# The attention output product of a mixer by seven products, its gate pairs regrouped, and the first three rows of w_o interleaved

## The chip, the cores and the metric

One core of a Trainium2 chip runs the whole program: TensorE (PE) multiplies, VectorE (DVE), ScalarE (ACT) and GpSimd (POOL) do the element work, and SyncE (SP) issues most of the loads. The metric is the device time of one execution in microseconds. Before the change the median of three executions is 2502.44 us (2501.37 to 2502.45).

## What is computed

Two layers of a macaron block over 640 tokens (512 of a new stream, 8 x 16 of running streams), 1024 features, float32:

```python
x += 0.5 * swiglu(rmsnorm(x) * g1, w_ffn1)
h  = rmsnorm(x) * gm
z  = h @ w_in                       # conv B | C | V | q | k | v | gates (2 x 1024)
y_conv = B * causal_conv3(C * V)    # 512 features
y_attn = band_attention(q, k, v)    # 512 features
m  = sigmoid(g_c) * (y_conv @ w_conv_out) + sigmoid(g_a) * (y_attn @ w_attn_out)
x += m @ w_o
x += 0.5 * swiglu(rmsnorm(x) * g2, w_ffn2)
```

and a last norm. The change lies in the computation of `m` and in `m @ w_o`.

## The kernel before

Everything is kept transposed: features on the 128 partitions, tokens (T = 640, in two halves of HT = 320) along the free dimension. Features come in tiles of 128 (KT = 8 of the model's width, CT = 4 of the conv's and of the attention's). Float32 products are made of three matmuls: each operand is split in a rounded part `hi` and a rest `lo`, and hi·hi + lo·hi + hi·lo is summed in PSUM. Weights arrive by SP in raw slabs of 128 x 1024 (`load`, a ring of three buffers); `prep` casts a slab to `whi` on ACT, and `flush` computes `wlo = raw - whi` on VectorE (L311). Both have rings of three.

Many products are done **by seven**: a product of 2 x 2 blocks (the two token halves, and odd and even feature tiles) is formed from seven block products instead of eight. The seven operands are named X11, X21, XN6, XT5, XT7, X22, XT4; those with N or T are sums of halves of the input. The weights' sums are made on VectorE in `source` (L250, four adds for a pair of slabs), whose results are split like raw slabs. One such stretch uses four slabs, s0 to s3, with two blocks of 12 matmuls in each of the first three and one in the last.

`outputs` is the part at issue. It holds, in this order, gate pairs 2, 4 and 6 (`gate_pair(m)`: rows m and m + 1 of the gates by seven, 84 matmuls into three PSUM banks qa, qb, qc); two `unit`s, which compute four rows each of y_conv @ w_conv_out by seven (84 matmuls; A and B are two-bank tiles, C two single banks); then gate pairs 8, 10, 12 and 14, and after each of these two rows of y_attn @ w_attn_out in the plain way (`out`, 48 matmuls a row, `py`). For gates from 8 on (`direct`), VectorE adds the blocks straight out of PSUM; for the others ACT copies a block to a scratch tile (`capsm`, `c`) and a DMA issued from POOL adds it (`accumulate`). `scale` multiplies a gate by the norm's factor `rrm`, `bend` is the sigmoid on ACT, `weigh` multiplies a row of the conv result by its gate, and `give` splits rows of `m` into hi and lo for w_o. Jobs are attached to numbered places of a pair or unit with `at(place, i, job)`; `spot` runs them there.

In this part the order on TensorE, VectorE and ACT is the one in which the program is written (`manual_schedule`, ORDERED), and each engine takes its queue strictly in that order, so an operation that waits holds up what is written behind it. The rows of `m @ w_o` follow: `product(po, mo)` for m = 0 to 7, 48 matmuls each, which need all eight rows of `mo` in turn; then x[m] is updated, and the next norm and the FFN's operands are begun (`ex.weights`, `ex.final`).

`mixer_order` lists the same pieces for the host, which packs the weights in the order of their use; `kinds` derives the slabs from it.

## Time and profile before

| | |
|---|---|
| median of three executions | 2502.44 us |
| the profiled execution | 2501.53 us |
| its span, from the first to the last instruction | 2499.7 us |
| granted TensorE clock | 0.999 |
| from gate pair 8 to the first row of w_o, layer 0 | 704.83 to 782.36 us |
| the same, layer 1 | 1940.3 to 2017.9 us |
| POOL busy in the first of these stretches | 0.00 us |

Times in the views count from the span's start. A row of the timeline gives start, length, engine, line, operation, result and operands, and in brackets the idle time before it with what ended that. Rows that overlap by some 0.08 us on one engine follow each other without a gap, so what an operation costs its engine is the distance from its start to the next one's. [...] The windows give an engine's busy time in a stretch. The chain is the work that ended last, followed back from the end.

### The profile page before, as it was taken

Reading aid. Unit: us, or ns where it says so; the run is one execution under the profiler, and the core shown is the slowest. Engines: PE = TensorE matmul, PEld = TensorE weight load, DVE = VectorE, ACT = ScalarE, POOL = GpSimd, SP = SyncE. Lnnn points to the kernel's source line nnn. Section 1 sums busy time; section 2 is a strip of 40 time slices with the busy share of each in tenths; the row PEclk is TensorE's granted clock in tenths of the full one; section 3 lists DMA queues with packets and bytes.
Section 4 is the critical chain, followed back from the end, with each engine's and each line's share of the span. In section 5 each row is a group of like instructions: output and inputs, shape, how many; then the busy total and the mean of one; then the engine's idle time right before and its main releaser. Section 6 shows DMA issues by size and latency. Waiting matters only on the chain.

```text
span 2499.7 us, 43407 instructions
## 1 busy us (share of the span) xinstructions
PE 2483.1 (99%) x17096; PEld 2425.8 (97%) x17096; DVE 2103.9 (84%) x3304; ACT 1418.8 (57%) x2281; POOL 335.3 (13%) x407
## 2 busy tenths in 40 slices
PE   9999999999999999999999999999999999999998
PEld 8999999888999999999999999998899999999998
DVE  7888888878886899888798889888788868989887
ACT  7455556664654555555565555556646455555554
POOL 0011211211100011111001111121111000111111
PEclk9999999999999999999999999999999999999999
DMA  4245665335323344666435565643344233565564
GB/s 146 82 109 122 138 138 130 108 108 172 101 76 112 95 119 119 137 135 135 114 92 128 129 133 121 138 119 117 132 145 107 78 114 94 119 132 120 131 135 111
DMA packets 127021, 299.59 MB, mean 120 GB/s; under 512 B 12160, under 2 KB 70912, under 8 KB 126816
## 3 DMA queue, kind: packets, MB, share of 16 engines
q1 hardware_dynamic: 68976, 219.18, 27.8%
q0 software_dynamic: 57120, 76.98, 18.5%
q8 instruction: 134, 2.20, 0.4%
q10 hardware_dynamic: 720, 0.65, 0.1%
q14 instruction: 71, 0.58, 0.1%
HBM read 221.13 MB, written 7.94 MB: 92 GB/s over the span
## 4 chain that ended last, share of the span: by engine, by line
PE 94%; DVE 3%; ACT 2%; DMA 0%; issue 0%; SPq 0%; DVEq 0%
PE pab L396 12%; PE paa L396 11%; PE pcb L396 6%; PE pca L396 6%; PE daa L963 5%; PE dab L963 5%; PE po L373 4%; PE qa L396 4%; PE pbb L396 3%; PE pba L396 3%; PE dca L963 3%; PE dcb L963 3%; PE pda L373 2%; PE pv L1589 2%; PE ma_cv L396 2%; PE qc L396 2%
## 5 line engine op out<-in xcount | busy, mean ns | idle before, releaser
L311 DVE TENSOR_TENSOR wlo<-raw,whi 128x1024 fp32r<-128x1024 f32 (+1 forms) x575 | 593.7, 1035 | 222.9 <-ACT whi L306 217.4
L306 ACT CAST whi<-raw 128x1024 fp32r<-128x1024 f32 (+1 forms) x575 | 515.6, 900 | 349.3 <-PE pbb L396 44.6
L306 ACT CAST whi<-s 128x1024 fp32r<-128x1024 f32 (+1 forms) x160 | 151.1, 945 | 246.5 <-issue 107.9
L396 PE MATMUL pab<-xhib,whi 128*128 128x320 f32 x704 | 218.3, 310 | 0.4 <-DVE gb L250 0.4
L396 PE MATMUL pab<-xlob,whi 128*128 128x320 f32 x704 | 217.4, 309 | 0.0
L396 PE MATMUL pab<-xhib,wlo 128*128 128x320 f32 x704 | 217.4, 309 | 0.0
L396 PE MATMUL paa<-xhia,whi 128*128 128x320 f32 x640 | 198.1, 310 | 0.2 <-DVE ga L250 0.2
L396 PE MATMUL paa<-xloa,whi 128*128 128x320 f32 x640 | 197.7, 309 | 0.0
L396 PE MATMUL paa<-xhia,wlo 128*128 128x320 f32 x640 | 197.7, 309 | 0.0
L311 DVE TENSOR_TENSOR wlo<-s,whi 128x1024 fp32r<-128x1024 f32 (+1 forms) x160 | 174.0, 1088 | 10.6 <-ACT whi L306 10.6
L396 PEld LDWEIGHTS pab<-xhib,whi 128*128 128x128 f32 x704 | 132.1, 188 | 1.1 <-DVE gb L250 0.9
L396 PEld LDWEIGHTS pab<-xlob,whi 128*128 128x128 f32 x704 | 132.1, 188 | 0.2
L396 PEld LDWEIGHTS pab<-xhib,wlo 128*128 128x128 f32 x704 | 132.1, 188 | 0.0
L396 PEld LDWEIGHTS paa<-xhia,whi 128*128 128x128 f32 x640 | 120.2, 188 | 0.5 <-DVE ga L250 0.5
L396 PEld LDWEIGHTS paa<-xloa,whi 128*128 128x128 f32 x640 | 120.1, 188 | 0.1
L396 PEld LDWEIGHTS paa<-xhia,wlo 128*128 128x128 f32 x640 | 120.1, 188 | 0.0
L250 DVE TENSOR_TENSOR raw<-raw,raw 128x512 f32<-128x512 f32 x160 | 109.5, 684 | 1.3
L250 DVE TENSOR_TENSOR raw<-s,raw 128x512 f32<-128x512 f32 x160 | 109.7, 686 | 0.0
L396 PE MATMUL pcb<-xhib,whi 128*128 128x320 f32 x352 | 108.7, 309 | 0.0
L396 PE MATMUL pcb<-xlob,whi 128*128 128x320 f32 x352 | 108.7, 309 | 0.0
L396 PE MATMUL pcb<-xhib,wlo 128*128 128x320 f32 x352 | 108.7, 309 | 0.0
L987 POOL DMA_DIRECT2D x<-c_b x52 | 62.6, 1204 | 309.7 <-ACT c_b L980 134.6
(705 smaller groups left out, 8073.0 us busy)
## 6 DMA issues: line engine op xcount, KB each, us to landing
raw<-in_wst SPq DMA_DIRECT2D x375, 512.0 KB, 3.7
x<-c_b POOLq DMA_DIRECT2D x52, 320.0 KB, 5.0
x<-c_a POOLq DMA_DIRECT2D x50, 320.0 KB, 5.1
kc<-in_kcache SPq DMA_DIRECT2D x32, 256.0 KB, 3.7
vc<-in_vcache SPq DMA_DIRECT2D x16, 512.0 KB, 4.5
ub<-cbb POOLq DMA_DIRECT2D x42, 160.0 KB, 6.0
ua<-cba POOLq DMA_DIRECT2D x38, 160.0 KB, 5.3
x<-u_a POOLq DMA_DIRECT2D x18, 320.0 KB, 5.1
```

The source lines that it names most:

```text
L250: DVE.tensor_tensor(out=out, in0=a, in1=b, op=ALU.add)
L306: ACT.copy(hi[:, d], src[:, c])
L311: DVE.tensor_tensor(out=lo, in0=src, in1=hi.bitcast(F32), op=ALU.subtract)
L373: PE.matmul(ps[:, a, :HT], w, x[:, a * HT : (a + 1) * HT], start=first and j == 0, stop=last and j == 2)
L396: PE.matmul(ps, a, b, start=start and kp == 0 and j == 0, stop=stop and kp == NP - 1 and j == 2, skip_group_check=True)
L963: PE.matmul(ps[u], w, y, start=start and i == 0 and j == 0, stop=i == 1 and j == 2, skip_group_check=True)
L987: POOL.dma_start(rows(r, cols), z, accum_op=ALU.add)
L1589: PE.matmul(pv[t], xx[:, t * P : (t + 1) * P], w[:, kk * AW : (kk + 1) * AW], start=c == 0 and kk == 0 and j == 0, stop=c == KT // 2 - 1 a ...
```

## The change

The attention's output product goes by seven, through the same `unit` as the conv's, generalised by a name ("co", "ao") and by the class `Inputs`, which makes the sums of its input. The order becomes gates 8, 10, 12, unit ao 0, gate 14, unit ao 4. The results of the units stay in the tile of y_attn (`yas`); `join(m)` multiplies a row by its gate and adds it to the conv's row, for rows 0 to 3 by an accumulating DMA, for rows 4 to 7 on VectorE. The `direct` branch goes: all gate pairs use ACT's copy and POOL's accumulating DMA, and so does the z part of every unit but the last. `give` is split in a job for the hi parts (ACT) and one for the lo parts (`gave`, VectorE). Gates 12 and 13 live with 4 to 7 in one tile `held`.

In the w_o product the first three rows are done together, input by input: inputs 0 and 1 for rows 0, 1 and 2, then 2 and 3, then 4, then 5 for rows 0 and 1, then 6 and 7 for row 0, for row 1, and 5 to 7 for row 2. Row 2 uses two single PSUM banks (`po_2a`, `po_2b`).

```diff
 def mixer_order():
...
-    for i, g in enumerate(gates[4:]):
-        out += [g, ("ao", 2 * i), ("ao", 2 * i + 1)]
+    out += gates[4:7] + [("unit", ("ao", 0)), gates[7], ("unit", ("ao", 4))]
...
+            pos = [acc(f"po{l}_{m}") for m in range(2)]
+            pos.append([att(f"po{l}_2{i}")[:, :HT] for i in "ab"])
+            ws = [[tiles.take() for _ in range(KT)] for _ in pos[:2]]
+            third = quiet()
+            ws.append([tuple(z[:, k * P : (k + 1) * P] for z in third) for k in range(KT)])
+            for ms, ks in (((0, 1, 2), (0, 1)), ((0, 1, 2), (2, 3)), ((0, 1, 2), (4,)), ((0, 1), (5,)),
+                           ((0,), (6, 7)), ((1,), (6, 7)), ((2,), (5, 6, 7))):
+                for m in ms:
+                    for k in ks:
+                        multiply(pos[m], ws[m][k], mo[k], k == 0, k == KT - 1)
             for m in range(KT):
-                po = acc(f"po{l}_{m}")
-                product(po, mo)
+                if m < len(pos):
+                    po = pos[m]
+                else:
+                    po = acc(f"po{l}_{m}")
+                    product(po, [mo[k] for k in range(KT)])
+                if m == 1:
+                    prep(len(ready))
                 ex.weights(m)
-                DVE.tensor_tensor(out=halves(x[m]), in0=two(po), in1=halves(x[m]), op=ALU.add)
+                if m == 2:
+                    for a in range(2):
+                        add(halves(x[m])[:, a], po[a], halves(x[m])[:, a])
+                else:
+                    DVE.tensor_tensor(out=halves(x[m]), in0=two(po), in1=halves(x[m]), op=ALU.add)
...
+        held = gp.tile([P, CT, T], F32, name=f"gt{l}")
+
         def gate_pair(m):
...
             def take(out, ps, c):
-                if direct:
-                    add(out, ps, out)
-                else:
-                    ACT.copy(c, ps)
-                    accumulate(out, c)
+                ACT.copy(c, ps)
+                accumulate(out, c)
...
             copy(z, -1.0)
+            spot(me, 4)
+            if not last:
+                accumulate(rows(1, t2), z)
             flush()
             ahead()
             mul(C, s2, 1, X22, False)
             for i in range(2):
                 add(rows(0, t2)[:, i], C[i], rows(0, t2)[:, i])
-            add(rows(1, t2), rows(1, t2), z)
+            if last:
+                add(rows(1, t2), rows(1, t2), z)
...
+        def join(m):
             def job():
-                for c in cs:
-                    ACT.copy(ya[c][0], yas[:, c, :])
+                y = yas[:, m % CT]
+                times(y, gates[KT + m])
+                if m < CT:
+                    accumulate(mm[m], y)
+                else:
+                    add(mm[m], mm[m], y)
             return job
...
+        at("g8", 1, second.opening)
+        at("g8", 2, second.firsts)
+        at("g8", 3, second.raw_low(0))
+        at("g8", 5, second.raw_low(1), weigh(4))
+        at("g10", 1, second.lasts)
+        at("g10", 2, scale(8))
+        at("g10", 4, second.sum_high(0))
+        at("g10", 5, second.sum_high(1), weigh(5))
+        at("g12", 1, second.sum_low(0))
+        at("g12", 2, second.sum_low(1))
+        at("g12", 3, scale(10))
+        at("g12", 4, bend(8))
+        at("ao0", 3, scale(12))
+        at("ao0", 5, bend(10), join(0))
+        at("g14", 1, join(2))
+        at("g14", 2, join(1))
+        at("g14", 3, join(3))
+        at("g14", 5, weigh(6, 7), bend(12))
+        at("ao4", 2, give(0, 1))
+        at("ao4", 3, gave(0, 1))
+        at("ao4", 4, give(2, 3))
+        at("ao4", 5, gave(2, 3))
         for m in (2, 4, 6):
             gate_pair(m)
-        unit(0, yc)
-        unit(CT, spare)
-        for m in range(0, KT, 2):
-            gate_pair(m + KT)
-            last = m == KT - 2
-            out(m, (lambda: give(range(3))) if last else None)
-            out(m + 1, (lambda: give(range(3, 6))) if last else None)
-        give(range(6, KT))
+
+        unit("co", 0, yc)
+        unit("co", CT, spare)
+        for m in (8, 10, 12):
+            gate_pair(m)
+        unit("ao", 0, yas)
+        gate_pair(14)
+        unit("ao", CT, yas, True)
+        join(4)()
+        give(4)()
+        scale(14)()
+        bend(14)()
+        for m in (5, 6, 7):
+            join(m)()
+            give(m)()
+            gave(m - 1)()
+        gave(7)()
```

How this moves the instructions, at three places of layer 0. First VectorE in gate pair 10 (`g_10` is a gate, `qa`, `qb`, `qc` its PSUM banks, `py` a plain row, `ya` the attention's result, `gt` the tile `held`). Before, with two rows of plain product done in between:

```order
L250 TENSOR_TENSOR raw_7892<-s_105_7931,raw_7892 128x512
L311 TENSOR_TENSOR wlo_8014<-raw_7892,whi_8013 128x1024
L250 TENSOR_TENSOR g_10_7997<-qb_10_7995,g_10_7997 128x320
L311 TENSOR_TENSOR wlo_8031<-raw_7929,whi_8030 128x512
L1291 TENSOR_TENSOR mm_7138<-mm_7138,g_4b 128x640
L1291 TENSOR_TENSOR mm_7138<-mm_7138,g_6b 128x640
L250 TENSOR_TENSOR g_10_1_7998<-qa_10_7994,g_10_1_7998 128x320
L311 TENSOR_TENSOR wlo_8065<-raw_8062,whi_8064 128x1024
L250 TENSOR_TENSOR g_10_7997<-qc_10_7996,g_10_7997 128x320
L1291 TENSOR_TENSOR g_10_1_7998<-g_10_1_7998,rrm_4681 128x320
L1291 TENSOR_TENSOR g_10_7997<-g_10_7997,rrm_4681 128x640
L1343 TENSOR_TENSOR g_10_1_7998<-qa_10_7994,rrm_4681 128x320
```

After, from the same sum on:

```order
L249 TENSOR_TENSOR raw_7866<-s_104_7891,raw_7866 128x512
L310 TENSOR_TENSOR wlo_7950<-raw_7866,whi_7949 128x1024
L1398 TENSOR_TENSOR ya_4623<-ya_4623 128x2x320
L1400 SCALAR_TENSOR_TENSOR ya_4623<-ya_4623 128x2x320 x2
L310 TENSOR_TENSOR wlo_7969<-raw_7889,whi_7968 128x512
L1309 TENSOR_TENSOR g_8_7800<-g_8_7800,rrm_4681 128x640
L1309 TENSOR_TENSOR g_8_1_7801<-g_8_1_7801,rrm_4681 128x320
L310 TENSOR_TENSOR wlo_8003<-raw_8000,whi_8002 128x1024
L249 TENSOR_TENSOR raw_8000<-raw_8000,raw_8023 128x512
L249 TENSOR_TENSOR s_106_8025<-raw_8000,raw_8023 128x512
L249 TENSOR_TENSOR raw_8023<-raw_8023 128x512
L1353 TENSOR_TENSOR g_10_1_7934<-qa_10_7930,rrm_4681 128x320
```

The three adds from the banks of pair 10 are gone; the sums of `ya` and the scaling of gates 8 and 9 stand in their place, and the weight sums for pair 12 follow inside the pair, where before they stood in the plain rows behind it.

Second, ACT around the beginning of gate pair 14, after the change (`aao_0` is bank pair A of unit ao 0, `sm` holds the sigmoid's bias, `capsm` and `c` are the scratch tiles). The copy into `g_14` comes behind the sigmoids of gates 10 and 11 and ahead of two casts:

```order
L1435 ACTIVATE ya_4623<-aao_0_8194 128x2x320
L1132 ACTIVATE g_10_7933<-g_10_7933,sm 128x640
L1132 ACTIVATE g_10_1_7934<-g_10_1_7934,sm 128x640
L1329 COPY g_14_8329<-qa_14_8326 128x320
L305 CAST whi_8344<-raw_8260 128x1024
L305 CAST whi_8362<-raw_8282 128x512
L1337 COPY g_14_8329<-qa_14_8326 128x320
```

Before, there was no unit ahead of pair 14, and no result of one was multiplied by a gate whose buffer `g_14` takes.

Third, VectorE at the passage to w_o. Before:

```order
L1476 TENSOR_TENSOR g_14_8375<-py_6_8493,g_14_8375 128x640
L250 TENSOR_TENSOR mm_7138<-mm_7138,g_14_8375 128x640
L311 TENSOR_TENSOR wlo_8497<-raw_8494,whi_8496 128x1024
L221 TENSOR_TENSOR m_3lo<-yc_4682,m_3hi 128x640
L221 TENSOR_TENSOR m_4lo<-mm_7138,m_4hi 128x640
L221 TENSOR_TENSOR m_5lo<-mm_7138,m_5hi 128x640
L1476 TENSOR_TENSOR g_14_1_8376<-py_7_8538,g_14_1_8376 128x640
L250 TENSOR_TENSOR mm_7138<-mm_7138,g_14_1_8376 128x640
L221 TENSOR_TENSOR m_6lo<-mm_7138,m_6hi 128x640
L221 TENSOR_TENSOR m_7lo<-mm_7138,m_7hi 128x640
```

After (twelve rows from the adds of C of unit ao 4 on; the products for rows 5 to 7 of `m` follow in the same manner):

```order
L249 TENSOR_TENSOR ya_4623<-c1ao_4_8464,ya_4623 128x320
L249 TENSOR_TENSOR ya_4623<-ya_4623,capsm_4680 128x2x320
L310 TENSOR_TENSOR wlo_8578<-raw_8560,whi_8577 128x1024
L1504 TENSOR_TENSOR m_2lo<-yc_4682,m_2hi 128x640
L1504 TENSOR_TENSOR m_3lo<-yc_4682,m_3hi 128x640
L1309 TENSOR_TENSOR ya_4623<-ya_4623,gt_7139 128x640
L310 TENSOR_TENSOR wlo_8644<-raw_8580,whi_8643 128x1024
L249 TENSOR_TENSOR mm_7138<-mm_7138,ya_4623 128x640
L1309 TENSOR_TENSOR g_14_8329<-g_14_8329,rrm_4681 128x640
L1309 TENSOR_TENSOR g_14_1_8330<-g_14_1_8330,rrm_4681 128x320
L1309 TENSOR_TENSOR ya_4623<-ya_4623,gt_7139 128x640
L249 TENSOR_TENSOR mm_7138<-mm_7138,ya_4623 128x640
```

Four rows of `m` (4 to 7) are now finished after the last unit instead of two, and the lo parts of three slabs of w_o are wanted in the same stretch. On TensorE the 48 matmuls of `po_0` stood in one run; now 12 of `po_0`, 12 of `po_1` and 12 of row 2 take turns.

More of the change, by code (lines that the diff above doesn't have):

```diff
@@ L1295, in gate_pair @@
             pa, pb, pc = (att(f"q{i}{n}")[:, :HT] for i in "abc")
-            direct = m >= KT
-            if m in (4, 6):
-                u, g = (gp.tile([P, T], F32, name=f"g{n}{i}") for i in "ab")
+            if m in (4, 6, 12):
+                u, g = held[:, m % 4], held[:, m % 4 + 1]
             else:
@@ L1400, in unit @@
+        def unit(name, m0, to, last=False):
+            n = f"{name}{l}_{m0}"
+            A, B = (acc(f"{i}{n}") for i in ("ba" if m0 else "ab"))
             if m0:
                 A, B = B, A
[L1402 removed]
+            C = [att(f"c{i}{n}")[:, :HT] for i in range(2)]
             a, b = ([z[:, i, :HT] for i in range(2)] for z in (A, B))
[L1404 removed]
+            me = f"{name}{m0}"
             def mul(ps, s, half, kind, start):
@@ L1460, in weigh @@
             return job
-        def parts(pool, tag, name, src):
-            hi, lo = (pool.tile([P, T], F32R, tag=f"{tag}{i}", name=f"{name}{i}") for i in ("hi", "lo"))
-            split(hi, lo, src)
-            return hi, lo
-        ya, mo = [], []
-        def out(m, then=None):
-            py = acc(f"py{l}_{m}")
-            product(py, ya)
-            if then:
-                then()
-            g = gates[m + KT]
-            DVE.tensor_tensor(out=halves(g), in0=two(py), in1=halves(g), op=ALU.mult)
-            add(mm[m], mm[m], g)
-            flush()
@@ new lines, in give, with gave, job @@
+            return job
+        def gave(*ms):
+            def job():
+                for m in ms:
+                    hi, lo = mo[m]
+                    DVE.tensor_tensor(out=lo, in0=mm[m], in1=hi.bitcast(F32), op=ALU.subtract)
+            return job
+        first, second = Inputs(yc), Inputs(yas)
+        at("g2", 1, first.opening)
+        at("g2", 2, first.firsts)
+        at("g2", 3, first.raw_low(0))
+        at("g2", 5, first.raw_low(1))
+        at("g4", 1, first.lasts)
+        at("g4", 3, first.sum_high(0))
```

112 lines of the change are left out of this document (43 added, 69 removed).

## The prediction

> **What bounds the kernel now.** I read the page first (busy shares, then the chain that ended last), then two windows, the gate pairs with the two w_conv_out units and the gate pairs with w_attn_out, and then the waits of TensorE.
>
> ```profile
> span 2499.7 us, 43407 instructions
> ...
> PE 2483.1 (99%) x17096; PEld 2425.8 (97%) x17096; DVE 2103.9 (84%) x3304; ACT 1418.8 (57%) x2281; POOL 335.3 (13%) x407
> ...
> PE 94%; DVE 3%; ACT 2%; DMA 0%; issue 0%; SPq 0%; DVEq 0%
> ...
> core 0: us, PE busy (x) PEld busy (x) DVE busy (x) ACT busy (x) POOL busy (x), PEclk, DMA share, GB/s
> 643.00:704.80 61.80, 61.73 (x419) 61.20 (x418) 51.82 (x73) 40.88 (x67) 7.82 (x9) 1.00 0.41 110
> 704.83:782.36 77.53, 77.53 (x531) 77.53 (x530) 63.01 (x91) 37.33 (x56) 0.00 (x0) 1.00 0.28 89
> ```
>
> TensorE is the bound: 99% of the span, 94% of the chain, and in the second window, which is the stretch that the change rebuilds in layer 0, it is busy for all of 77.53 us at full clock. VectorE has 14.5 us of that window free, so the question is not its total but whether its operands come in time. The first window matters because it already holds the pattern that the second will get: three gate pairs, then units by seven, with accumulating DMAs from POOL. There TensorE was busy 61.73 of 61.80 us with VectorE at 84%.
>
> **What is removed on TensorE.** A product row of w_attn_out is one piece of the chain:
>
> ```profile
> 717.34 7.04 PE py L373 x48
> ...
> L373 PE MATMUL py<-xhi,whi x128: 306/308/312, 717.2 to 2017.1; 128*128 128x320 f32 x128
> ```
>
> 48 matmuls in 7.04 us are 0.1467 us each (the mean of 308 ns is the length of one, not its pitch). The second row is one of three alike (hi·hi, lo·hi, hi·lo): 384 matmuls, 192 in a layer. Seven products of a quarter instead of eight leave 168 in a layer, so 24 go: 24 × 0.1467 = **3.52 us a layer**. They stood on a TensorE without gaps, so all of it shortens the path, unless operands come later.
>
> **A wait that goes.** TensorE's waits in and behind these windows, as the weight loads show them, and the matmuls around the last:
>
> ```profile
> PEld po L373 <- DVE m_6lo L221: 0.3, 1, 0.3
> PEld bco L1413 <- ACT yc L1420: 0.3, 1, 0.3
> PEld aco L1413 <- ACT mm L1420: 0.3, 1, 0.3
> ...
> 787.64 0.46 PE L373 MATMUL po<-m_6hi,whi 128*128 128x320 f32 x2
> 788.18 0.56 PE L373 MATMUL po<-m_6lo,whi 128*128 128x320 f32 x2
> 788.58 0.45 PE L373 MATMUL po<-m_6hi,wlo 128*128 128x320 f32 x2
> ```
>
> Two matmuls take 0.29 us; here 0.54 and 0.40 pass, so a wait costs its length, 0.25, and about 0.1 more until the flow is back: 0.36 in all. The other two belong to the passage from one w_conv_out unit to the next, which stands in the same order after the change, so they stay.
>
> **Does VectorE keep up in the pairs?** The adds of the gates (`direct`) leave it; a copy on ACT and an accumulating DMA take their place. Two products with gates that were read out of PSUM now go through `join`, half of them by DMA. Added on it are the sums of weight quarters and of y (`Inputs(yas)`). The third pair before gives the price of each operation as start to start:
>
> ```profile
> 657.44 0.68 DVE L250 TENSOR_TENSOR raw<-s,raw 128x512 f32<-128x512 f32 x1
> 659.29 1.22 DVE L311 TENSOR_TENSOR wlo<-raw,whi 128x1024 fp32r<-128x1024 f32 x1 [1.17 <-ACT whi L306]
> 660.43 0.82 DVE L1383 TENSOR_TENSOR yc<-yc 128x640 f32<-128x640 f32 x1
> ...
> 667.45 0.49 DVE L1343 TENSOR_TENSOR g_4b<-qa,rrm 128x320 f32<-128x320 f32 x1 [0.62 <-PE qa L396]
> ...
> 672.06 1.48 DVE L1371 TENSOR_TENSOR xlo<-yc,xhi 128x1280 fp32r<-128x1280 f32 x1
> 673.47 0.69 DVE L311 TENSOR_TENSOR wlo<-raw,whi 128x512 fp32r<-128x512 f32 x1
> 674.07 1.49 DVE L1371 TENSOR_TENSOR xlo<-yc,xhi 128x1280 fp32r<-128x1280 f32 x1
> 675.47 1.22 DVE L1291 TENSOR_TENSOR g<-g,rrm 128x640 f32<-128x640 f32 x2
> 676.61 1.22 DVE L311 TENSOR_TENSOR wlo<-raw,whi 128x1024 fp32r<-128x1024 f32 x1
> 677.86 0.69 DVE L250 TENSOR_TENSOR raw<-raw,raw 128x512 f32<-128x512 f32 x1
> ...
> 679.80 0.48 DVE L1343 TENSOR_TENSOR g_6b<-qa,rrm 128x320 f32<-128x320 f32 x1
> 680.20 0.68 DVE L311 TENSOR_TENSOR wlo<-s,whi 128x512 fp32r<-128x512 f32 x1
> 680.80 0.69 DVE L311 TENSOR_TENSOR wlo<-raw,whi 128x512 fp32r<-128x512 f32 x1
> ...
> 679.60 0.31 PE L1413 MATMUL aco<-xhi,whi 128*128 128x320 f32 x1
> ```
>
> The reader sees a cycle of 12.35 us (667.45 to 679.80). Prices: 1.14 for 1024 columns, 1.41 for 1280, 0.60 for 512, 0.40 for 320, 0.74 for 640 (that many columns by the same slope), 1.14 for `scale`, 1.94 for three sums of weights (677.86 to 679.80), and 1.85 from the fourth sum to the lo part that needs ACT's cast of it.
>
> Pair 10 holds what pair 4 held, and `weigh(4)` (0.74) and `scale(8)` (1.14), less the 0.62 in which VectorE waited at its end: 1.26 late. Pair 12 is as pair 6, plus `weigh(5)`, 0.74: about 1.9 late at the unit (adding up every row gives 1.84). In the unit before, the lo part for its third block of matmuls was ready at 681.49; TensorE starts the unit at 679.60, comes to that block after 24 matmuls (+3.52) and to the lo part two later: 683.41. That is 1.92 of slack, so the lateness just uses it up: I take 0.1 of wait. In pair 12 ACT's queue is the nearer one:
>
> ```profile
> 667.39 1.26 ACT L1368 CAST xhi<-yc 128x1280 fp32r<-128x1280 f32 x1
> ...
> 669.22 0.43 ACT L1313 COPY g_6a<-qa 128x320 f32<-128x320 f32 x1 [0.56 <-PE qa L396]
> ...
> 670.78 0.31 PE L396 MATMUL qa<-thi,whi 128*128 128x320 f32 x1
> ```
>
> The copy of the first block ended 1.13 before TensorE wrote that bank again; 1.1 to 1.26 late, with the same cast ahead of it, it costs 0.1.
>
> **A new wait in pair 14.** Its u takes the buffer of g_8, so ACT's first copy waits for `join(0)`, a VectorE multiply. On VectorE, from the sums' end (2.04 into unit ao0): 0.40 + 1.20 (two lo parts) + 1.85 + 1.14 + 0.60 + 0.74 (add of B) + 1.14 (`scale(12)`) + 1.25 + 1.94 + 0.80 (adds of C) + 1.80 (fourth sum, two lo parts) + 0.74 = 13.6, so at 15.65. With 0.1 to ACT and 0.43 of copy it is 16.2; TensorE wants the bank at 12.35 + 3.52 = 15.87. Wait 0.3. Queued behind the copy on ACT is the cast for the pair's third slab, due 3.5 us later, which does not suffer. I take 0.35 with the refill; bounds 0 and 0.8.
>
> **The tail.** Unit ao4 ends at 12.33 from its own start. Its C is read by VectorE from 10.77; behind that stand 0.40, 0.82 (z), 1.14 (lo of w_o row 1), 1.48 (m_2, m_3), 0.74 and 1.22 (lo of row 2): 16.6. TensorE, with two inputs for each of rows 0 and 1 first, wants row 2's lo part at 12.33 + 3.52 + 0.59 = 16.44: 0.2 with the refill. Row 1 takes the bank of A, which ACT frees behind a cast (0.95) and its copy (0.6 to 0.7): 14.1 to 14.2, against 14.09: 0.2. Of m_6, twelve operations later (9.6), VectorE is done at 26.2; the interleaving lets TensorE come to it at 12.33 + 14.96 = 27.3. So the wait of 0.36 for m_6 goes, while in the old order it would stand there after 36 matmuls, at 12.33 + 5.28 = 17.6, and wait 8.6. Weights of row 3 need a cast and a lo part after row 0 is done, 2.2 us, under 4.4 us of rows 1 and 2. VectorE's work on x[0] to x[2] is bunched; before, it waited some 2.3 us in every row of w_o, which takes that up:
>
> ```profile
> 804.03 0.82 DVE L1214 TENSOR_TENSOR x<-po,x 128x640 f32<-128x640 f32 x1 [2.28 <-PE po L373]
> ```
>
> **POOL and the DMAs.** Nineteen more accumulating DMAs a layer, twelve for gates, three for z, four for joins. Loads from HBM are the same in number.
>
> ```profile
> 676.58 0.85 POOL L1288 DMA_DIRECT2D g_6a<-capsm  x1 [8.54 <-ACT capsm L1308]
> 677.13 1.18 POOL L1288 DMA_DIRECT2D g_6b<-c  x1
> 678.81 0.86 POOL L1288 DMA_DIRECT2D g_6a<-capsm  x1 [0.50 <-DVE raw L250]
> ...
> DMA to landing us min/median/max: 2.8/3.4/4.9
> ...
> raw<-in_wst SPq DMA_DIRECT2D x10, 512.0 KB, 3.3
> ```
>
> A pair's last is issued some 11.6 us into it, and lands at most 4.9 later, at 16.5; `scale(8)` comes 9.3 into the next pair, at 21.6. Hidden by 5 us; the other two scales likewise. Weight loads in the window with these DMAs landed in 3.3 us. Cost: nothing, and if the cover goes, VectorE's queue stands, and with it the lo parts behind.
>
> [...]
>
> **The sum**, a layer: −3.52 − 0.36 + 0.1 + 0.1 + 0.35 + 0.2 + 0.2 = −2.93; both layers −5.9. The span goes from 2499.7 to 2493.8. The profiled execution took 2501.53, 1.8 around the span, and is 0.9 under the median of the three runs, so on the median: 2502.44 − 5.9 = **2496.5**. Bounds: with no new wait −7.8, 2494.7; with each new wait doubled −3.88 + 1.9, −4.0 in two layers, 2498.5.
>
> **Rivals.**
>
> First, the new waits all vanish in slack, 2494.7. For it: the first window, the same pattern, ran with 0.07 us of idle TensorE. Against: pairs 10 and 12 are heavier than 4 and 6.
>
> Second, VectorE becomes the bound of the stretch. If operations cost their lengths (0.82 rather than 0.74) because each waits for the one before, some 17 in pair 10, 15 in pair 12 and 17 in unit ao0 add 1.4 + 1.2 + 1.4 = 4 us, all past the slack: −3.88 + 0.95 + 4 = +1.1 a layer, 2504.6; half of it is 2500.5. Against: independent operations followed each other at 0.74 and 0.60 in these rows.
>
> Third, slower: POOL's issues and VectorE shut each other out. Nineteen issues of some 1 us are 19 us of VectorE in a stretch that has about 8 to spare (74 us of TensorE against some 66 of work by the prices above): +11 −3 = +8 a layer, 2518. It decides from about half of each issue on. Against: the rows at 676.61 and 659.29.
>
> That the products stay eight is no rival: the order of TensorE holds 48 matmuls fewer.
>
> **How the numbers follow.** What a measurement here can tell from no change is about 0.2%, 5 us: faster means under 2497.4. Chances: the forecast 0.50 (0.44 faster, 0.06 same; its own range 2495.3 to 2497.8), the first rival 0.15 (faster), doubled waits 0.16 (same), VectorE as the bound 0.11 (0.09 same, 0.02 slower), POOL 0.08 (0.07 slower, 0.01 same). Faster 0.59, same 0.32, slower 0.09. The range 2494.0 to 2501.0 leaves out POOL's case, the worse half of VectorE's and a little below the full gain.
>
> **What would show it.** 48 matmuls fewer; the stretch from pair 8 to the first w_o matmul 74.0 us plus 0.5 or so; TensorE's waits naming ACT's copy in pair 14, ACT's copy of A at row 1 and the lo part at row 2, none of them over 0.5; no wait for m_6. Wrong it is if waits of TensorE name the lo parts in pair 12 or unit ao0 with more than 0.5 (second rival), if accumulations land after 9 us or VectorE's rows beside POOL grow (third), or if the gain reappears as a loss in the rows of w_o or the FFN behind.

## The result, and the profile after

| | before | after |
|---|---|---|
| median of 14 executions each, on one chip | 2501.86 us (2501.37 to 2502.49) | 2496.68 us (2496.15 to 2497.16) |
| ratio, 95% interval | | 0.9979 (0.9971 to 0.9987) |
| span of the profiled execution | 2499.7 us | 2494.7 us |
| gate pair 8 to the first row of w_o, layer 0 and layer 1 | 77.53, 77.53 us | 74.52, 74.53 us |
| first row of w_o to the first matmul on `pab` behind it | 66.50, 66.50 us | 66.86, 66.38 us |

The change makes the kernel 5.2 us faster, 0.21%. Forecast were 5.9, and 2496.5 us. The time is met more closely (0.2 us) than the gain (0.7), because the forecast started from 2502.44 us, the median of three executions, and the longer series of the same kernel has 2501.86: that part is luck.

Each run below was taken with a series of its own of the kernel before, and the ratios refer to that series. The medians of these series lie between 2501.59 and 2501.97 us, so a difference in microseconds between a run and the changed kernel is good to some 0.3 us. One of the seven executions of the run with the four edits took 13114.83 us; its ratio leaves it out.

The page of the changed kernel, first the span, then busy time and instructions of each engine, then the chain that ended last:

```profile
span 2494.7 us, 43515 instructions
...
PE 2478.1 (99%) x17048; PEld 2419.0 (97%) x17048; DVE 2119.2 (85%) x3322; ACT 1450.0 (58%) x2343; POOL 370.7 (15%) x445
...
PE 94%; DVE 3%; ACT 2%; DMA 1%; issue 0%; SPq 0%; DVEq 0%; ACTq 0%
```

TensorE has 48 matmuls fewer and is still the bound. VectorE has 15 us more work, ACT 31, POOL 35. The windows of the changed kernel have the columns named before the forecast (length, busy time of PE, PEld, DVE, ACT and POOL, granted clock, DMA share, GB/s). The first two are the rebuilt stretch and the rows of w_o with the start of the FFN, both in layer 0; the third is the rebuilt stretch of layer 1.

```profile
705.00:779.52 74.52, 74.38 (x506) 73.89 (x505) 65.18 (x91) 48.90 (x81) 15.27 (x17) 1.00 0.59 141
779.52:846.38 66.86, 66.52 (x457) 66.17 (x455) 52.21 (x72) 37.77 (x50) 5.17 (x6) 1.00 0.39 105
...
1938.10:2012.63 74.53, 74.43 (x506) 73.99 (x505) 65.49 (x92) 48.88 (x81) 15.27 (x17) 1.00 0.59 142
```

VectorE now fills 65.18 of 74.52 us, 87%, where it filled 63.01 of 77.53. The stretch is 3.0 us shorter in both layers; the 24 matmuls that went from it are worth 3.52. The other half microsecond, and what TensorE waits for behind the stretch, shows in the waits of the weight loads, here of layer 0 (total us, times, longest):

```profile
PEld po L372 <- ACT ya L1435: 0.6, 1, 0.6
PEld qa L395 <- ACT g L1329: 0.4, 1, 0.4
PEld bco L1428 <- ACT yc L1435: 0.3, 1, 0.3
...
PEld aco L1428 <- ACT mm L1435: 0.3, 1, 0.3
PEld qa L395 <- ACT gt L1329: 0.2, 1, 0.2
```

Two of these five (bco, aco) are the waits at unit co4 that the kernel before has as well. New are, from below, pair 12, pair 14 and row 1 of w_o. The wait for m_6 is gone. To size a wait I take TensorE's timeline and subtract 0.1467 us a matmul from the distance between two starts. Row 1 and row 2 in layer 0:

```profile
780.99 0.46 PE L372 MATMUL po<-m_1hi,wlo 128*128 128x320 f32 x2
781.78 0.56 PE L372 MATMUL po<-m_0hi,whi 128*128 128x320 f32 x2 [0.34 <-ACT ya L1435]
782.18 0.45 PE L372 MATMUL po<-m_0lo,whi 128*128 128x320 f32 x2
...
784.23 0.41 PE L372 MATMUL po_2a<-m_0hi,wlo 128*128 128x320 f32 x1
784.47 0.31 PE L372 MATMUL po_2b<-m_0hi,wlo 128*128 128x320 f32 x1
```

Two matmuls are 0.29: from 780.99 to 781.78 that leaves 0.50 of wait, to 782.18 another 0.11 until the flow is back. At row 2 (784.23 to 784.47, one matmul) only such a refill of 0.09 is left: VectorE's lo part for this place ended at 784.17, just before.

```profile
782.95 1.22 DVE L310 TENSOR_TENSOR wlo<-raw,whi 128x1024 fp32r<-128x1024 f32 x1
```

The same subtraction at each place gives (wait and refill together, us, good to 0.02):

| place | priced | layer 0 | layer 1 |
|---|---|---|---|
| pair 12, second block | 0.1 | 0.22 | 0.17 |
| unit ao0, lo part | 0.1 | 0 | 0 |
| pair 14, second block | 0.35 | 0.40 | 0.36 |
| w_o row 1, bank of A | 0.2 | 0.61 | 0.10 |
| w_o row 2, lo part | 0.2 | 0.09 | 0.10 |
| sum | 0.95 | 1.32 | 0.73 |

With 3.52 + 0.36 gained, these waits leave 2.56 us for layer 0 and 3.15 for layer 1. Measured are 2.65 (3.01 gained in the first stretch, 0.36 lost in the second) and 3.12 (3.00 + 0.12). Together that is 5.77, against 5.86 forecast. The span shrank by only 5.0: the three parts outside these stretches (up to pair 8 of layer 0, between the stretches, and behind the last) ran 0.17, 0.26 and 0.34 us longer. The 0.17 arises in the first 14 us of the program, ahead of all that was changed, and 0.27 of the 0.34 between its last two matmuls (0.59 us apart, 0.32 in the kernel before). Why is open; the 14 executions of the changed kernel differ by up to 1.01 us, those of the kernel before by up to 1.12.

### The profile page after: what moved, and what is told of

It is laid out like the page before. It is cut to its first block, busy times and chain, and to the rows that moved or that the text cites. A ratio compares the mean times of both kernels' runs of the same rounds, so it can differ in the third digit from the quotient of the medians.

```text
span 2494.7 us, 43515 instructions
## 1 busy us (share of the span) xinstructions
PE 2478.1 (99%) x17048; PEld 2419.0 (97%) x17048; DVE 2119.2 (85%) x3322; ACT 1450.0 (58%) x2343; POOL 370.7 (15%) x445
## 4 chain that ended last, share of the span: by engine, by line
PE 94%; DVE 3%; ACT 2%; DMA 1%; issue 0%; SPq 0%; DVEq 0%; ACTq 0%
PE pab L395 12%; PE paa L395 11%; PE pcb L395 6%; PE pca L395 6%; PE daa L962 5%; PE dab L962 5%; PE po L372 4%; PE qa L395 4%; PE pbb L395 3%; PE pba L395 3%; PE dca L962 3%; PE dcb L962 3%; PE pda L372 2%; PE pv L1622 2%; PE ma_cv L395 2%; PE qc L395 2%
## 5 line engine op out<-in xcount | busy, mean ns | idle before, releaser
L310 DVE TENSOR_TENSOR wlo<-raw,whi 128x512 fp32r<-128x512 f32 (+1 forms) x583 | 598.6, 1030 | 236.1 <-ACT whi L305 230.6
L305 ACT CAST whi<-raw 128x512 fp32r<-128x512 f32 (+1 forms) x583 | 519.9, 897 | 348.0 <-PE pbb L395 44.6
```

What stands on the lines that cost most here:

```text
L305: ACT.copy(hi[:, d], src[:, c])
L310: DVE.tensor_tensor(out=lo, in0=src, in1=hi.bitcast(F32), op=ALU.subtract)
```

## Which parts of the change carry it

**The rows of w_o in the old order.** The changed kernel, with the units by seven, but w_o row after row:

```diff
-            pos = [acc(f"po{l}_{m}") for m in range(2)]
-            pos.append([att(f"po{l}_2{i}")[:, :HT] for i in "ab"])
...
-            for ms, ks in (((0, 1, 2), (0, 1)), ((0, 1, 2), (2, 3)), ((0, 1, 2), (4,)), ((0, 1), (5,)),
-                           ((0,), (6, 7)), ((1,), (6, 7)), ((2,), (5, 6, 7))):
...
             for m in range(KT):
...
+                po = acc(f"po{l}_{m}")
+                product(po, [mo[k] for k in range(KT)])
```

> The changed kernel with the rows of w_o taken one after the other, each with all eight inputs. Our theory: the interleaving hides the wait for the last four mixed inputs. In the changed kernel the lo parts of m_4 to m_7 are ready 787.6 to 793.1 us into the span, 8 to 13.5 us after the first matmul of w_o, while row 0 alone reaches m_4 after 24 matmuls, 3.5 us. So TensorE waits in row 0, for m_4 to m_7 in turn, about 8 us a layer; the waits at rows 1 and 2 (0.7 and 0.2 us in the two layers) go. 2496.7 + 12 to 16 = 2509 to 2513 us, ratio to the kernel before 1.003 to 1.0045: slower than before. Rival, that the interleaving is no part of the gain because VectorE's order would adjust: 2496 to 2498, ratio 0.998. Between the two, 2501 to 2506, would mean that m_4 to m_7 come earlier when the lo part of row 2 and the cast for it are not ahead of them.

Measured: 2511.25 us, ratio to the kernel before 1.0039 (1.0024 to 1.0054). The interleaving is worth 14.6 us to the changed kernel. Waits of the weight loads in layer 0:

```profile
PEld po L372 <- DVE m_4lo L1485: 2.4, 1, 2.4
PEld po L372 <- ACT m_4hi L1478: 1.6, 1, 1.6
PEld po L372 <- DVE m_5lo L1485: 0.8, 1, 0.8
PEld po L372 <- DVE m_6lo L1485: 0.8, 1, 0.8
```

TensorE stands in row 0 for one input after the other, at VectorE's pace: the lo parts of m_4 to m_7 start at 786.30, 788.63, 790.96 and 791.83 there. From the second of these waits on it also ran at half clock (0.50 between 787 and 793 us; the last section shows the window). In waits, refills and slow steps it lost 8.1 us in layer 0 and 8.7 in layer 1. In the changed kernel the same four lo parts are no earlier. VectorE's timeline has them at:

```profile
787.56 0.82 DVE L1504 TENSOR_TENSOR m_4lo<-mm,m_4hi 128x640 fp32r<-128x640 f32 x1
...
789.89 0.82 DVE L1504 TENSOR_TENSOR m_5lo<-mm,m_5hi 128x640 fp32r<-128x640 f32 x1
...
792.22 0.82 DVE L1504 TENSOR_TENSOR m_6lo<-mm,m_6hi 128x640 fp32r<-128x640 f32 x1
793.10 0.83 DVE L1504 TENSOR_TENSOR m_7lo<-mm,m_7hi 128x640 fp32r<-128x640 f32 x1
```

The reader sees that nothing made these operands earlier; row 1 and row 2, with the inputs that are there, fill the time.

**The interleaved rows alone.** The kernel before with that part of the change and no other:

```diff
-                po = acc(f"po{l}_{m}")
-                product(po, mo)
+            for ms, ks in (((0, 1, 2), (0, 1)), ((0, 1, 2), (2, 3)), ((0, 1, 2), (4,)), ((0, 1), (5,)),
+                           ((0,), (6, 7)), ((1,), (6, 7)), ((2,), (5, 6, 7))):
+                for m in ms:
+                    for k in ks:
+                        multiply(pos[m], ws[m][k], mo[k], k == 0, k == KT - 1)
```

> The kernel before with w_o's first three rows interleaved and nothing else. Our theory: there is only the wait for m_6 to gain, 0.36 us a layer, and row 1 writes a bank that VectorE reads late (the last product of w_attn_out, multiplied by its gate only 2 to 2.5 us after TensorE wants the bank), so it costs up to 2 us a layer: 2502 to 2506, ratio 1.000 to 1.002. Rival, that the interleaving by itself carries a good part of the gain: 2499 or less, ratio under 0.999.

Measured: 2509.10 us, 1.0028 (1.0017 to 1.0039), 7.5 slower than before and beyond the 2506 that I gave. TensorE's timeline, and VectorE's:

```profile
783.75 0.31 PE L373 MATMUL po<-m_1hi,wlo 128*128 128x320 f32 x1
786.36 0.56 PE L373 MATMUL po<-m_0hi,whi 128*128 128x320 f32 x2 [2.30 <-DVE g L1495]
```

```profile
785.48 0.82 DVE L1495 TENSOR_TENSOR g<-py,g 128x640 f32<-128x640 f32 x1
```

Row 1 writes the bank of the last row of w_attn_out, and VectorE reads that bank at 785.48, behind lo parts. The place was right: a wait of 2.46 and a refill of 0.10 in layer 0, 2.46 in layer 1. What I had not priced is the clock afterwards. The windows behind the wait, layer 0 and layer 1 (the granted clock is the third number from the end):

```profile
786.30:790.00 3.70, 3.64 (x25) 3.64 (x26) 3.44 (x5) 0.73 (x1) 0.00 (x0) 1.00 0.36 134
2024.00:2027.40 3.40, 3.32 (x12) 3.32 (x13) 3.34 (x5) 0.73 (x1) 0.00 (x0) 0.51 0.35 107
```

In layer 1 TensorE came back at half clock for 3.4 us and lost 1.6 more (12 matmuls in 3.37 us in place of 1.76). So layer 0 lost 2.56 − 0.36 (m_6) = 2.2 and layer 1 2.46 + 1.6 − 0.36 = 3.7, together the 5.9 by which this span (2505.6) is longer than the one before. The execution that was profiled is the fastest of the eight, 2507.33; the median lies 1.8 above it. Half clock behind the wait of layer 0 too would make 1.6 of that, but no trace shows such an execution.

The two halves of the change are thus no independent gains: units alone are 9.7 us slower than the kernel before, interleaved rows alone 7.5 slower, both together 5.2 faster. The units, with their joins, delay the last inputs of w_o, and the interleaving covers that; the interleaving wants the bank of row 1 early, and a unit's bank is freed by ACT where the old product's was freed late by VectorE.

**Two rows in place of three.**

```diff
-            pos.append([att(f"po{l}_2{i}")[:, :HT] for i in "ab"])
...
-            for ms, ks in (((0, 1, 2), (0, 1)), ((0, 1, 2), (2, 3)), ((0, 1, 2), (4,)), ((0, 1), (5,)),
-                           ((0,), (6, 7)), ((1,), (6, 7)), ((2,), (5, 6, 7))):
+            for ms, ks in (((0, 1), (0, 1)), ((0, 1), (2, 3)), ((0, 1), (4,)), ((0, 1), (5,)),
+                           ((0,), (6, 7)), ((1,), (6, 7))):
```

> The changed kernel with only rows 0 and 1 of w_o interleaved by inputs; row 2 is a row like the others, so its cast and lo part are not ahead of the last mixed inputs. Our theory: the order covers exactly as much as it delays m_4. Run one after the other, the rows had m_4 to m_7 ready at 787.0, 789.4, 791.7 and 793.5 us; two rows with four inputs take 48 matmuls, 7.0 us, and bring TensorE to m_4's lo part at 786.7, and the further ones at 1.8, 1.8 and 0.9 us distance. So it waits 0.3 + 0.5 + 0.3 + 0.6 and four refills of 0.1 to 0.2, 2.1 to 2.5 us a layer, in place of 0.7 and 0.2 at rows 1 and 2: 1.4 to 2.2 a layer lost against the changed kernel, 2499.5 to 2501.1 us, with the clock kept, since each wait is short. Rival, that two rows are enough: within 1 us of the changed kernel, 2497.7 or less. Rival, that waits of this kind halve the clock as in the run with the rows one after the other: over 2502.

Measured: 2501.01 us, 0.9996 (0.9987 to 1.0005). The third row is worth 4.3 us, most of the gain of the change (5.2). Waits in layer 1, and the window that holds them:

```profile
PEld po L372 <- DVE m_4lo L1497: 1.1, 1, 1.1
PEld po L372 <- DVE m_6lo L1497: 0.6, 1, 0.6
PEld po L372 <- DVE m_5lo L1497: 0.6, 1, 0.6
```

```profile
2023.00:2031.00 8.00, 6.55 (x41) 5.76 (x40) 6.94 (x10) 2.80 (x5) 0.00 (x0) 1.00 0.05 9
```

With refills these are 2.2 to 2.3 us a layer, as expected, though divided otherwise (m_4 longer, m_7 none). Three waits of 1.1, 0.6 and 0.6 us leave the clock at 1.00 in this window. The wait at row 1, which I thought would go, stayed (0.90 in layer 0): it does not hang on the third row but, as shown below, on ACT's queue.

## Does VectorE keep up, and do POOL's issues hurt it

**Adds on VectorE.** The changed kernel, with the blocks of pairs 8 to 14 added from PSUM as the kernel before did:

```diff
             def take(out, ps, c):
-                ACT.copy(c, ps)
-                accumulate(out, c)
+                if m >= KT:
+                    add(out, ps, out)
+                else:
+                    ACT.copy(c, ps)
+                    accumulate(out, c)
```

> The changed kernel with the three blocks of each gate pair 8 to 14 added by VectorE straight from PSUM, as the kernel before did, in place of ACT's copies and POOL's accumulating DMAs: 12 VectorE operations of 0.40 us a layer more, 1.2 us a pair; ACT loses 12 copies and POOL 12 DMAs. Our theory: VectorE has about 1.9 us of slack at the unit after pair 12 and it is used up, so 2.4 to 3.6 us of lateness more become waits of TensorE for lo parts in pairs 10 and 12, in the unit and in pair 14: 2 to 4 us a layer, 2501 to 2505 us, ratio 1.000 to 1.0015. Rival, that VectorE has room (its lateness is taken up by waits of its own): 2496 to 2498, ratio 0.998. Rival, that POOL's issues hold VectorE up in the changed kernel: faster than 2495.

Measured: 2503.00 us, 1.0006 (0.9997 to 1.0016): 6.3 lost, 3.2 a layer, the middle of what was expected. The waits of the weight loads in layer 0, and VectorE around the first of them:

```profile
PEld qa L395 <- DVE gt L249: 1.9, 1, 1.9
PEld qa L395 <- DVE g L249: 1.6, 1, 1.6
```

```profile
727.65 1.22 DVE L1309 TENSOR_TENSOR g<-g,rrm 128x640 f32<-128x640 f32 x2
728.78 0.48 DVE L249 TENSOR_TENSOR g<-qb,g 128x320 f32<-128x320 f32 x1
729.18 0.48 DVE L249 TENSOR_TENSOR g<-qa,g 128x320 f32<-128x320 f32 x1
```

The two large waits are not for lo parts, as I had expected, but for the bank of qa, which VectorE frees at 729.6 behind `scale(8)`; in layer 1 they are 1.4 and 1.8 us long. So ACT's copies do two things: they take 1.2 us a pair off VectorE, and they free the bank from another queue. This run cannot divide the loss between the two. It shows that VectorE, in its present order, could not take these adds back, and that the 24 DMAs that replace them pay.

**Twice the issues.**

```diff
-            POOL.dma_start(out, z, accum_op=ALU.add)
+            n = out.shape[-1] // 2
+            for c in (slice(0, n), slice(n, 2 * n)):
+                POOL.dma_start(out[..., c], z[..., c], accum_op=ALU.add)
```

> The changed kernel with each accumulating DMA of the mixer's gates, units and joins split in two of half the size: the same bytes, twice the issues on POOL. Our theory: POOL is 15% busy and nobody waits for its issues, so 2496 to 2497.5 us, ratio 0.998. Rival, that issues on POOL and VectorE's instructions shut each other out, or that the accumulations land only just in time: each further issue of about 1 us would hold VectorE up, some 50 issues a layer, and the time grows by 5 us or more, ratio over 1.000. The length of VectorE's instructions beside the issues tells it as well: 1.22 us for the lo part of 1024 columns in our theory, longer in the rival.

Measured: 2496.74 us, 0.9980 (0.9971 to 0.9990): no change. Groups of instructions of this kernel, VectorE from 705 to 779.5 us and POOL from 700 to 785 (times, busy us and mean ns):

```profile
L310 DVE TENSOR_TENSOR wlo<-raw,whi 128x1024 fp32r<-128x1024 f32 x12 | 14.7, 1224 | 6.5 <-ACT whi L305 6.5
```

```profile
L1308 POOL DMA_DIRECT2D g<-capsm x12 | 15.0, 1595 | 16.5 <-ACT capsm L1326 16.0 <-DMA yc<-ya 0.5
```

The lo part of 1024 columns lasts 1224 ns on average in this run, 1222 in the changed kernel, 1218 in the kernel before, which had no issue in this stretch. The rows that had an issue running beside them are no longer than the others: 1223 against 1225 ns here, 1219 against 1223 in the changed kernel. POOL was busy with issues for 33.2 of the 85 us from 700 to 785, against 16.5 in the changed kernel, and the trace shows no other engine waiting for them. So the third rival is out: for issues of this kind the measurement shows no lock between POOL and VectorE. One thing this run leaves open: in its profiled execution the two weight slabs at w_o in layer 0 landed 1.0 us later after their issue than in the changed kernel's, and row 1 waited 1.26 us instead of 0.50. The medians do not differ, so whether the issues have a part in that is not shown.

## The waits that are left

**The copy that frees row 1's bank.** ACT in layer 0 and in layer 1 of the changed kernel:

```profile
780.08 1.06 ACT L305 CAST whi<-raw 128x1024 fp32r<-128x1024 f32 x1 [0.51 <-DMA raw<-in_wst]
781.04 0.69 ACT L1435 ACTIVATE ya<-aao 128x640 f32<-128x640 f32 x1
```

```profile
2012.69 1.05 ACT L305 CAST whi<-raw 128x1024 fp32r<-128x1024 f32 x1 [0.48 <-PE aao L1428]
2013.64 0.70 ACT L1435 ACTIVATE ya<-aao 128x640 f32<-128x640 f32 x1
```

The copy stands behind a cast, as the forecast had it. In layer 0 that cast waited 0.51, by the profile for its weights from HBM, and began 0.56 after the first matmul of w_o (779.52); without this wait the copy would have ended at 781.2, in time for TensorE at 781.28. In layer 1 the cast began 0.06 after the first matmul (2012.63), and only a refill stands at row 1. The slab took 5.51 us from issue to landing in layer 0 and 4.05 in layer 1. Fifteen of its sixteen parts had landed by 778.18 in layer 0, the last at 779.70. Between 773 and 785 us the trace also has two transfers of instructions (16 and 8 KB), and none in the like stretch of layer 1, 2006 to 2018; that they delay the last part is not shown, nor is why the cast began only 0.38 after it. The edit puts the copy first, and with it VectorE's lo part for row 2 ahead of the first join:

```diff
         unit("ao", CT, yas, True)
+        prep(len(ready))
+        flush()
```

> The changed kernel with one swap on ScalarE: its copy of A in unit ao4, which frees the bank of w_o's row 1, stands ahead of the cast of the weights of w_o's row 2. Our theory: the copy was late only because it stood behind that cast, and the cast, in layer 0, behind a weight slab that landed late; so the wait at row 1 (0.5 and its refill of 0.1 in layer 0, 0.1 in layer 1) goes, at the price of a cast and a lo part for row 2 later by 0.6 to 0.7 us, which the lo part, behind VectorE's queue anyway, does not feel: at row 2 the 0.1 of refill stays or grows to 0.4. Span 0.3 to 0.7 us shorter than the changed kernel's, 2496.0 to 2496.5 us. Rival, that the copy waits for TensorE's last block of the unit or for a buffer: the wait at row 1 stays 0.5 or more in layer 0. Rival, that row 2 then waits in its place: 0.6 or more there and no gain.

Measured: 2495.87 us, 0.9976 (0.9967 to 0.9985). The wait at row 1 went in both layers; at row 2 0.30 stands with its refill in layer 0, and nothing in layer 1. The mechanism holds; the waits account for 0.6 of the 0.8 us of median.

**Pair 14's buffer.** What ACT's copy waits for in the changed kernel, and VectorE's multiply before it:

```profile
757.81 0.43 ACT L1329 COPY g<-qa 128x320 f32<-128x320 f32 x1 [0.73 <-DVE ya L1309]
```

```profile
756.90 0.82 DVE L1309 TENSOR_TENSOR ya<-ya,g 128x640 f32<-128x640 f32 x1
```

```diff
+            elif m == 14:
+                u, g = held[:, 2], tmp(f"g{n}_1")
...
-        at("g8", 3, second.raw_low(0))
+        at("g8", 3, second.raw_low(0), weigh(6))
...
-        at("g14", 5, weigh(6, 7), bend(12))
+        at("g14", 5, weigh(7), bend(12))
```

> The changed kernel with pair 14's u in a buffer of its own (that of gate 6's product, whose multiplication is brought forward from pair 14 to pair 8), so that ScalarE's first copy in pair 14 does not wait for the join with gate 8. Our theory: the wait of 0.30 and 0.25 us with refill of 0.1 in pair 14 goes in both layers, and nothing comes in its place but 0.74 us of VectorE work earlier, in pair 8, which has the slack: span 0.6 to 0.9 us shorter, 2495.8 to 2496.3 us. Rival, that the copy in pair 14 is late for another reason (the cast ahead of it on ScalarE, as in pair 12): the wait stays over 0.2 in both layers. Rival, that VectorE has nothing to spare in pair 8: waits of 0.5 or more in pairs 10 and 12.

Measured: 2495.07 us, 0.9974 (0.9963 to 0.9985). The wait in pair 14 is gone in both layers, pair 12's is 0.27 in both, and at row 1 only the refill stands. The edit takes away 0.76, and pair 12 gives 0.13 of it back; the rest of the 1.6 is in row 1 of layer 0, where 0.5 less is lost (its weights came in time here), and in scatter. So this run shows the cause of pair 14's wait, but its median moved by more than the edit accounts for.

**Unit co0's copy.** Two waits, together 0.59 us a layer, that the change left alone:

```diff
-            s3 = slab(True)[0]
+            early = me == "co0"
+            if early:
+                flush()
+                s3 = quiet()
+            else:
+                s3 = slab(True)[0]
             ahead()
             mul(a, s3, 0, XT4, False)
             copy(rows(1, t1), -1.0)
+            if early:
+                prep(used[0] + 1)
...
-        at("co0", 5, bend(6))
+        at("co4", 3, bend(6))
```

> The changed kernel with unit co0's last copy of A ahead of the two casts for the next unit on ScalarE, and one step of the weights moved with it. The change left this place alone, and both kernels have waits of TensorE there for the banks of B and A when unit co4 begins, 0.22 + 0.11 and 0.16 + 0.10 us a layer. Our theory: the two copies stand behind casts, so the swap takes these waits away, 0.59 us a layer, and the span is 0.9 to 1.2 us shorter than the changed kernel's, 2495.4 to 2496.0 us. Rival, that they are the length of a copy behind the last matmul and no order takes them away: the span as in the changed kernel. Rival, that the casts are then late: TensorE waits for the first weights of unit co4, 0.6 us or more.

Measured: 2496.16 us, 0.9977 (0.9968 to 0.9986). The two waits are gone, but the sigmoids moved into unit co4 delay ACT there, and a wait of 0.15 + 0.10 stands at its last copy. That nets 0.7 in two layers, less than the 0.9 to 1.2 expected; the median moved by 0.5.

**All of them.** The three edits, and a fourth for pair 12: the cast of 1280 columns behind the first copy.

```diff
-        at("g10", 5, second.sum_high(1), weigh(5))
-        at("g12", 1, second.sum_low(0))
+        at("g10", 5, weigh(5))
+        at("g12", 1, second.sum_high(1), second.sum_low(0))
```

> The changed kernel with the three edits of the other runs together (the copy of A in unit ao4 ahead of a cast, pair 14's u in a buffer of its own, unit co0's copy ahead of two casts) and a fourth: the cast of 1280 columns that stands ahead of ScalarE's first copy in pair 12 is moved behind it. Our theory: these are the waits that TensorE still has between unit co0 and w_o, 1.8 us in layer 0 and 1.3 us in layer 1 with their refills, and each has its own cause, so the gains add up: 2.0 to 3.0 us, 2493.6 to 2494.8 us, ratio to the kernel before 0.997. Rival, that one wait taken away moves the lateness to the next place (VectorE is behind throughout): the span under 1 us shorter, 2495.7 or more.

Measured: 2495.18 us, 0.9973 (0.9962 to 0.9984): 1.5 gained where 2 to 3 were expected. Every wait of the list went, but a new one stood in pair 12, 0.57 and 0.10 in both layers, and the 0.15 and 0.10 of unit co4 stayed. ACT in pair 12:

```profile
731.64 0.42 ACT L1331 COPY gt<-qa 128x320 f32<-128x320 f32 x1
734.11 1.05 ACT L305 CAST whi<-raw 128x1024 fp32r<-128x1024 f32 x1 [2.05 <-DVE raw L249]
735.06 1.26 ACT L1376 CAST xhi<-ya 128x1280 fp32r<-128x1280 f32 x1
736.22 0.62 ACT L305 CAST whi<-raw 128x512 fp32r<-128x512 f32 x1
736.74 0.42 ACT L1339 COPY gt<-qa 128x320 f32<-128x320 f32 x1
```

The moved cast did not go into the 2.05 us in which ACT waits, but behind the instruction that waits, and so ahead of the next copy of qa. The last run puts it right behind the first copy, and the two sigmoids behind the third copy of unit co4:

```diff
             ACT.copy(u[:, t1], pa)
+            spot(me, 0)
             prep(used[0] + 1)
...
-        at("g12", 1, second.sum_high(1), second.sum_low(0))
+        at("g12", 0, second.sum_high(1))
+        at("g12", 1, second.sum_low(0))
...
-        at("co4", 3, bend(6))
+        at("co4", 4, bend(6))
```

> The run with the four edits together, with two of them placed better. There the cast of 1280 columns in pair 12 came to stand behind the cast for the pair's second slab and ahead of the copy of its third block (a wait of 0.57 + 0.10 us of TensorE in both layers); it now stands right behind the first copy, where ScalarE was idle for 2.05 us. And two sigmoids that had been moved into unit co4 stand behind its third copy of A instead of ahead of it (0.15 + 0.10). Our theory: these 0.92 us a layer go and at most 0.3 us at w_o's row 2 come back, since VectorE then is 0.7 us later against TensorE: span 2491.4 to 2492.4, 2493.3 to 2494.3 us, 2.4 to 3.4 us faster than the changed kernel, ratio to before 0.9967. Rival, that the waits move on (to the lo parts in pair 12, pair 14 or row 2): a span of 2493 or more, as before this placing.

Measured: 2493.57 us, 0.9966 (0.9954 to 0.9978). Its slowest execution (2494.55) is under the fastest of the changed kernel, so it beats both kernels: 8.4 us under the before of its own series, where the changed kernel has 5.2. Windows over much the same two stretches of layer 0:

```profile
705.00:779.00 74.00, 74.00 (x505) 73.88 (x504) 65.39 (x92) 49.17 (x82) 15.23 (x17) 1.00 0.59 140
779.00:846.00 67.00, 67.00 (x462) 67.00 (x460) 52.76 (x73) 38.18 (x50) 5.17 (x6) 1.00 0.40 108
```

TensorE is busy throughout; one refill of 0.1 us in unit ao0 is left in each layer, and nothing came back at row 2. VectorE's work is the same as in the changed kernel (2119.9 and 2119.2 us), so what the four edits changed was order, not work. From unit co0 to w_o's row 2 TensorE lost 1.93 us in layer 0 of the changed kernel and 1.35 in layer 1, and here 0.09 in each: that is 3.1 us, and the median fell by 3.1.

## Why the prediction was right

- **24 matmuls a layer at 0.1467, 3.52.** Confirmed: 17096 became 17048, and the stretch shortened by that less its waits.
- **The wait for m_6, 0.36.** Gone in both layers. That the interleaving does it is shown by the run with the old order. The 8.6 us a layer that the forecast gave for this order are near the 8.1 and 8.7 that TensorE lost there, but not for its reason: there was not one wait for m_6 but four, two for m_4 and one each for m_5 and m_6, and part of the time was lost at half clock, which the forecast did not have. That the sizes agree is luck. The net cost, 7.3 us a layer, is smaller, in part because the waits at rows 1 and 2 go.
- **Unit ao0, 0.1.** No wait came, but it was near. VectorE had the lo part ready at 745.72 and TensorE came to it at 745.96: of the slack of 1.92, 1.68 was used. With the 0.23 that TensorE had just lost in pair 12 that makes 1.91, the lateness forecast. In the last run, without pair 12's wait, 0.11 was left.
- **Pair 12, 0.1.** The cause was named rightly (ACT's copy behind the cast of 1280 columns; the last run moves the cast behind the copy, and the wait is gone), and the size was 0.2, double.
- **Pair 14, 0.35.** 0.40 and 0.36. Freeing the buffer took it away, so the cause is shown.
- **Row 1, 0.2.** 0.61 and 0.10: the copy behind a cast was right, but I counted the cast from ACT's queue alone, and in layer 0 it stood 0.51 longer, by the profile for its weights. The term's mean, 0.36, is the largest miss of the sum. In layer 0 the wait alone, 0.50, is at the limit that the forecast set for a single one, and with its refill beyond it.
- **Row 2, 0.2.** 0.09 and 0.10, a refill and no more. In layer 0 row 1's wait had already given VectorE that time: TensorE came to the lo part at 784.23, 0.06 after it was done, and without the 0.61 lost at row 1 it would have come at 783.62. In the run with the copy first, where row 1 does not wait, 0.30 stands here.
- **The sum.** 0.95 of new waits a layer, measured 1.32 and 0.73. The misses cancel in part: that the total, 5.77 for 5.86, is better than its terms is luck.
- **POOL's DMAs at no cost.** No cost shows with twice the issues (2496.74 us against 2496.68). The bound on their landing was too short: I took at most 4.9 us, and the changed kernel's accumulating DMAs between 700 and 785 us show

```profile
DMA to landing us min/median/max: 3.1/4.8/8.3
```

In layer 1 the slowest took 9.1 us, past the 9 that the forecast named as a sign of its third rival. The long ones are three of the four joins and the gates of pair 14, and what reads them came 3.2 us or more after they had landed. The gates of pairs 8, 10 and 12, which the forecast's bound was made for, landed within 6.3 us, and their `scale` came 5.3 us or more after the last of them. So the cover of some 5 us was there, and nobody waited.

Of the rivals, VectorE as the bound was the near one: at 87% of the stretch it has room in total, but 1.2 us more a pair, with the banks freed by VectorE, cost 3.2 us a layer.

## What to carry to other kernels

Where a kernel's bound engine has no gaps, work removed from it is worth its full time only if the operands come as much earlier (here 3.52 us of work removed shortened the stretch by 3.0); the price is found by walking the queue of each engine that feeds it, and counting for each instruction what stands ahead of it, with the DMA it waits for. A rearrangement that delays operands and one that gives the bound engine something else to do in the meantime belong together: each alone made this kernel slower (by 9.7 and 7.5 us, where both together gain 5.2). An instruction moved into a queue's idle time must go ahead of the instruction that waits there, or it delays what stands behind that one (in pair 12 that cost TensorE 0.57 and 0.10 us a layer).

## What the hardware showed

The granted clock halved behind some waits of TensorE and stayed full behind others. In the run with the interleaved rows alone, one wait of 2.46 us with no matmul was followed by 0.51 of full clock for 3.4 us in layer 1, and the like wait of 2.46 us in layer 0 by full clock (1.00 from 786.3 to 790 us). The run with w_o's old order has a granted clock of 0.995 to 0.996 over whole executions, where the kernel before has 0.998 to 0.999. In its layer 1, waits of 1.19 and 2.31 us were followed by half clock, and in layer 0 waits of 1.52 and 2.31 us with two matmuls between them by this window:

```profile
787.00:793.00 6.00, 5.10 (x16) 4.31 (x17) 5.54 (x8) 1.59 (x3) 0.00 (x0) 0.50 0.00 0
```

Single waits of up to 1.80 us (the run with the adds on VectorE) did not do it: behind the two of layer 0 the granted clock was 1.00, from 729.7 to 733 and from 744 to 747 us. So the wait of 2.46 us in layer 1 cost 1.6 us more behind it, and the like wait in layer 0 no more than its refill of 0.10. Why these two differ, and whether a single wait between 1.80 and 2.46 us can do it, no run here shows.
